# Two more block-product pairs in an FFN's last projection, with their weight sums made earlier

## The chip, the cores and the metric

The kernel runs on one core of a Trainium2 chip. A core has five engines that work at the same time: TensorE (PE in the profile) multiplies matrices, VectorE (DVE) and ScalarE (ACT) do elementwise work, GpSimd (POOL) does elementwise work and can issue transfers, and SyncE (SP) issues most transfers. Each engine takes its instructions strictly in order; where one waits, all behind it on that engine wait too. The metric is the device time of one execution in microseconds (us), a median over runs.

## The reference

One layer of a streaming encoder on x of 512 tokens by 1024 features: a combined projection, an attention branch and a recurrent branch, a gated merge, and then the FFN, all in float32.

```python
hn = rmsnorm(h, norm_ffn_g[l])
gu = hn @ w_ffn_in[l]                      # 1024 -> 2 x 2816
g, up = jnp.split(gu, 2, axis=-1)
h = h + (jax.nn.silu(g) * up) @ w_ffn_out[l]   # 2816 -> 1024
return rmsnorm(h, final_norm_g)
```

The change concerns the last product, (silu(g) * up) @ w_ffn_out: 2816 = 22 tiles of 128 rows of w_ffn_out, taken as 11 pairs of two tiles.

## The kernel before

Float32 products are made from two reduced-precision parts. Every operand is split into a high part (ScalarE, L82: a copy that rounds) and a low part (VectorE, L83: the value less its high part), and a product takes three matmuls (L76 to L78, `mm3`): high by high, high by low, low by high. So each weight tile that arrives in a `raw` tile costs one ScalarE and one VectorE instruction before TensorE can read it as `whl`.

Some products are taken as block products, in the manner of Winograd's form of Strassen's scheme: the tokens, the inner dimension and the columns are halved, and seven products of half blocks, of sums of blocks, take the place of eight. In the FFN's last projection a pair of tiles holds the two inner halves. A plain pair takes 2 tiles x 4 token tiles x 2 column halves x 3 = 48 matmuls of 512 columns, a block-product pair 7 x 2 x 3 = 42. Before, pairs 0 to 4 are plain and 5 to 10 are block products (`N_PLAIN`). The block products need sums of weight blocks, t1 = b12 - b11, t2 = b22 - t1, t3b = b22 - b12 and t4 = b21 - t2 (`out_sums`, L223, L225, L231, L237: VectorE, 128 partitions x 512 each), and sums of activation blocks (`a_sums`, L1442 to L1445). Before, all of them are made in the last stage, between the matmuls that use them.

The stages that the change touches, in order of time:

- The loop over the recurrent branch (66 to 130 us): projections `xr`, `gr`, `ga`, `gb`, the causal convolution `xc` (VectorE, three taps, L725), the recurrence gates `rg` on TensorE (L759), which read `xch`, a low part that GpSimd makes of `xc` (L730). The tiles b0 to b3 of the pool `obp` hold blocks of another weight, w_o, whose sums are made there and kept in DRAM.
- The FFN units fg0, fu0, fg1, fu1, fg2, fu2 (to about 727 us): each is a block product over seven weight kinds in the order w11, t1, t2, w22, t3, w21, t4, with the sums t1, t2, t3, t4 made by VectorE (L352, L367, L373). The results of a unit `fu` multiply those of `fg` (`sg`), partly on GpSimd, and are transposed for the last projection.
- The last projection (728 us to the end): first column half (`po_out0`, `p_out`), then the second, then the final norm.

The order of TensorE is written out by hand in the FFN and in the last projection, that of VectorE in the loop and in the last projection; elsewhere a scheduler merges the engines' instructions. The order of the DMA queues follows the order of issue. The pool `tg` has two tiles; it holds only short-lived scratch.

Of the kernel before, what the change touches and what calls it, by code (L numbers as in the profile page):

```python
# [14 lines left out]
P = 128  # L15
# [18 lines left out]
N_PLAIN = 5  # L34
PAIR_TILES = 2 * (11 - N_PLAIN)


@with_exitstack
def block_kernel(ctx: ExitStack, tc: tile.TileContext, x, norm_mix_g, w_in, b_merge, rel_table,
# [103 lines left out]
    for i in plain[:-3]:  # L143
        plan_out(1, i)
    for i in paired:
        plan_block("t12", i)
    plan_out(1, plain[-3])
# [11 lines left out]
    def load(name, k):  # L159
# [4 lines left out]
        raw = wp.tile([P, n, wide], F32, tag="raw", bufs=3, name=f"raw_{name}_{k}")  # L164
# [12 lines left out]
    t2_of, t2_room = {}, []  # L177
# [17 lines left out]

    def out_sums(name, rows):

        kind, i = name.split("_")
        if kind == "t4":
# [5 lines left out]
        def half_row(col):  # L205
            o = out_room[0].tile([P, S], F32, tag="half", bufs=3, name=f"half_{name}")
            sp.dma_start(out=o[:], in_=w_ffn_out[rows + P:rows + 2 * P, col:col + S])
            return o[:]

        if kind == "t12":  # L210
            raw = wp.tile([P, 2, S], F32, tag="raw", bufs=3, name=f"raw_{name}")
            sp.dma_start(out=raw[:], in_=w_ffn_out[rows:rows + P, :].rearrange("p (c n) -> p c n", c=2))
            b22 = half_row(S)

            if len(t2_of) < 2:
                if not t2_of:
                    t2_room.append(spare[0].tile([P, 2, S], F32, tag="act", bufs=13, name="t2_room"))
                t2 = t2_room[0][:, len(t2_of)]
            else:
                t2 = out_room[0].tile([P, S], F32, name=f"t2_{i}")[:]  # L220
            t2_of[i] = t2
            t1 = raw[:, 1]
            dve.tensor_sub(t1, raw[:, 1], raw[:, 0])  # L223
            low_parts()
            dve.tensor_sub(t2, b22, t1)  # L225
            high_first(hl[:, 0, 1], hl[:, 1, 1], t1)
            high_first(hl[:, 0, 0], hl[:, 1, 0], t2)
        elif kind == "t3b":
            raw = wp.tile([P, 2, S], F32, tag="raw", bufs=3, name=f"raw_{name}")
            sp.dma_start(out=raw[:], in_=w_ffn_out[rows:rows + 2 * P, S:].rearrange("(k p) n -> p k n", p=P))  # L230
            dve.tensor_sub(raw[:, 0], raw[:, 1], raw[:, 0])  # L231
            low_parts()
# [626 lines left out]
    for j in range(0, KT, 2):  # L859
# [7 lines left out]
        if j:  # L867
            gates_of(j)
# [771 lines left out]
```

## Time and profile before

| what | value |
|---|---|
| time, median of 3 runs | 849.77 us (849.75 to 851.16) |
| the profiled execution | 849.69 us, span 847.9 us |
| TensorE busy | 839.1 us, 99% of the span, clock 0.999 |
| VectorE busy | 663.2 us, 78% |
| ScalarE busy | 522.5 us, 62% |
| GpSimd busy | 140.6 us, 17% |
| DMA | 137.17 MB, mean 162 GB/s |

The span is what the profiler recorded from the first to the last instruction; 849.69 - 847.9 = 1.8 us lie outside it. In rows of single instructions the columns are start (us), duration (us), engine, line, operation, the tile written and the tiles read, the shapes, and in brackets the idle time of the engine before the instruction with what ended it. A TensorE row lasts longer than the step to the next row, since matmuls overlap; the step between starts is what a matmul costs.

### The profile page before, as it was taken

Reading aid. Unit: us, or ns where it says so; the run is one execution under the profiler, and the core shown is the slowest. Engines: PE = TensorE matmul, PEld = TensorE weight load, DVE = VectorE, ACT = ScalarE, POOL = GpSimd, SP = SyncE. Lnnn points to the kernel's source line nnn. Section 1 sums busy time; section 2 is a strip of 40 time slices with the busy share of each in tenths; the row PEclk is TensorE's granted clock in tenths of the full one; section 3 lists DMA queues with packets and bytes.
Section 4 is the critical chain, followed back from the end, with each engine's and each line's share of the span. In section 5 each row is a group of like instructions: output and inputs, shape, how many; then the busy total and the mean of one; then the engine's idle time right before and its main releaser. Section 6 shows DMA issues by size and latency. Waiting matters only on the chain.

```text
span 847.9 us, 11598 instructions
## 1 busy us (share of the span) xinstructions
PE 839.1 (99%) x4114; PEld 710.8 (84%) x4114; DVE 663.2 (78%) x972; ACT 522.5 (62%) x864; POOL 140.6 (17%) x179
## 2 busy tenths in 40 slices
PE   9999999999999999999999999999999999999996
PEld 6988888888888888888888888888888999888885
DVE  6667769886999788787568777888778878798995
ACT  7595848774466688787534568654664576645434
POOL 2412030221050133333000000003002213200000
PEclk9999999999999999999999999999999999999999
DMA  8433386777545433222233974555544445526642
GB/s 284 167 104 118 128 298 234 221 266 247 186 137 150 112 100 101 87 75 75 64 110 125 342 295 132 187 163 159 161 152 148 132 138 178 162 75 210 211 137 99
DMA packets 95385, 137.17 MB, mean 162 GB/s; under 512 B 7288, under 2 KB 62160, under 8 KB 94816
## 3 DMA queue, kind: packets, MB, share of 16 engines
q1 hardware_dynamic: 93696, 132.93, 48.9%
q10 hardware_dynamic: 1232, 2.95, 0.9%
q8 instruction: 32, 0.52, 0.3%
q0 software_dynamic: 400, 0.57, 0.3%
q14 instruction: 25, 0.20, 0.1%
HBM read 122.75 MB, written 13.67 MB: 161 GB/s over the span
## 4 chain that ended last, share of the span: by engine, by line
PE 82%; DVE 8%; ACT 4%; DMA 3%; issue 2%; ACTq 0%; DVEq 0%
PE fu_x L78 2%; PE fu_x L76 2%; PE fu_x L77 2%; PE po_out L76 2%; PE po_out L77 2%; PE po_out L78 2%; PE o L1088 2%; PE fg_x L78 2%; PE fg_x L76 2%; PE fg_x L77 2%; PE pT L1068 2%; PE po_ga L78 2%; PE po_ya L78 2%; PE po_ya L77 2%; PE po_ya L76 2%
## 5 line engine op out<-in xcount | busy, mean ns | idle before, releaser
L1288 POOL TENSOR_TENSOR sg<-sg,keep_fu_x 128x512 f32<-128x512 f32 (+1 forms) x10 | 17.8, 1782 | 238.8 <-DVE keep_fu_x L1287 238.8
L1057 POOL TENSOR_SCALAR p<-p,rl 128x128 f32<-128x128 f32 (+3 forms) x61 | 44.0, 739 | 14.9 <-DVE rl L1053 14.0
L1051 DVE CUSTOM_DVE_ANT_0 p<-s,bias 128x128 f32<-128x128 f32 (+1 forms) x64 | 28.6, 485 | 11.6 <-PE s L1043 10.2
L1052 ACT ACTIVATE p<-p,m 128x128 f32<-128x128 f32 (+1 forms) x64 | 35.5, 556 | 2.4 <-DVE m L1051 2.0
L76 PE MATMUL po_out<-whl_fo,act_hi 128*128 128x512 f32 (+1 forms) x80 | 30.9, 386 | 0.0
L78 PE MATMUL po_out<-whl_fo,act_lo 128*128 128x512 f32 (+1 forms) x80 | 30.7, 384 | 0.0
L77 PE MATMUL po_out<-whl_fo,act_hi 128*128 128x512 f32 (+1 forms) x80 | 30.7, 384 | 0.0
L83 DVE TENSOR_TENSOR whl_fu_w<-raw_fu_w,whl_fu_w 128x1024 fp32r<-128x1024 f32 (+1 forms) x18 | 22.1, 1227 | 8.5 <-ACT whl_fu_w L82 8.5
L83 DVE TENSOR_TENSOR pp<-pT,pp 128x384 fp32r<-128x384 f32 (+1 forms) x48 | 26.9, 596 | 2.0 <-ACT pp L82 1.8
L77 PE MATMUL po_xr<-xnT,whl_xr 128*128 128x512 f32 (+1 forms) x80 | 27.7, 353 | 0.0
L83 DVE TENSOR_TENSOR whl_fu_t<-t_fu,whl_fu_t 128x1024 fp32r<-128x1024 f32 (+1 forms) x18 | 23.8, 1324 | 4.8 <-ACT whl_fu_t L82 4.6
L77 PE MATMUL po_gr<-xnT,whl_gr 128*128 128x512 f32 (+1 forms) x80 | 27.5, 347 | 0.0
L78 PE MATMUL po_gr<-xnT,whl_gr 128*128 128x512 f32 (+1 forms) x80 | 27.3, 347 | 0.0
L78 PE MATMUL po_xr<-xnT,whl_xr 128*128 128x512 f32 (+1 forms) x80 | 27.2, 346 | 0.0
L76 PE MATMUL po_gr<-xnT,whl_gr 128*128 128x512 f32 (+1 forms) x80 | 27.1, 347 | 0.0
L76 PE MATMUL po_xr<-xnT,whl_xr 128*128 128x512 f32 (+1 forms) x80 | 26.3, 351 | 0.4 <-ACT xnT L615 0.4
L83 DVE TENSOR_TENSOR whl_fo<-raw_fo,whl_fo 128x1024 fp32r<-128x1024 f32 x16 | 20.7, 1304 | 7.7 <-ACT whl_fo L82 7.7
L82 ACT ACTIVATE whl_fu_w<-raw_fu_w 128x1024 fp32r<-128x1024 f32 (+1 forms) x18 | 17.8, 989 | 13.0 <-issue 7.1
L76 PE MATMUL po_k<-xnT,whl_qk 128*128 128x512 f32 x64 | 25.5, 398 | 0.0
L76 PE MATMUL po_q<-xnT,whl_qk 128*128 128x512 f32 x64 | 25.5, 398 | 0.0
L76 PE MATMUL po_ga<-xnT,whl_ga 128*128 128x512 f32 x64 | 25.4, 397 | 0.0
L82 ACT ACTIVATE whl_fu_t<-t_fu 128x1024 fp32r<-128x1024 f32 (+1 forms) x18 | 17.7, 988 | 12.6 <-PE fu_x L78 9.0
(614 smaller groups left out, 2994.9 us busy)
## 6 DMA issues: line engine op xcount, KB each, us to landing
raw_qk<-in_w_in_dram SPq DMA_DIRECT2D x32, 256.0 KB, 3.2
raw_fu_w<-in_w_ffn_in_dram SPq DMA_DIRECT2D x16, 512.0 KB, 4.4
raw_fo<-in_w_ffn_out_dram SPq DMA_DIRECT2D x16, 512.0 KB, 4.1
raw_xr<-in_w_in_dram SPq DMA_DIRECT2D x8, 512.0 KB, 5.7
raw_gr<-in_w_in_dram SPq DMA_DIRECT2D x8, 512.0 KB, 4.4
raw_ga<-in_w_in_dram SPq DMA_DIRECT2D x8, 512.0 KB, 3.8
raw_gb<-in_w_in_dram SPq DMA_DIRECT2D x8, 512.0 KB, 3.6
o_b<-in_w_o_dram SPq DMA_DIRECT2D x8, 512.0 KB, 6.9
```

Source lines behind the costliest of these rows:

```text
L76: pe.matmul(o, sh, mh, start=start, stop=False, skip_group_check=parts)
L77: pe.matmul(o, sh, ml, start=False, stop=False, skip_group_check=parts)
L78: pe.matmul(o, sl, mh, start=False, stop=stop, skip_group_check=parts)
L82: act.activation(hi, src, AF.Copy)
L83: dve.tensor_sub(lo, src, f(hi))
L1051: dve.tensor_tensor_reduce(prob[qb][:], scs[qb][:, 0:w], bias[:, S - w:S], -1.0, 3e38, ALU.add, ALU.min, nmax[:, qb:qb + 1])
L1052: act.activation(prob[qb][:], prob[qb][:], AF.Exp, bias=nmax[:, qb:qb + 1], scale=-1.0, accum_out=lsum[:, qb:qb + 1])
L1057: eng.tensor_scalar(prob[qb][:], prob[qb][:], rl[:, qb:qb + 1], 1.0, ALU.mult, ALU.mult)
L1068: pe.transpose(pt[:, at * P:(at + 1) * P], prob[qb][:, kb * P:(kb + 1) * P], ident[:])
L1088: pe.matmul(po[:, S - n:S], st, pp[i][:, part, lo:lo + n], start=kb == 0 and part == 0, stop=kb == NT - 1 and part == 1)
L1288: (pool if keep and (unit != f_units[-1] or side) else dve).tensor_mul(o, o, keep[a] if keep else banks[a])
```

## The change

Pairs 3 and 4 become block products too, so that eight of eleven pairs are. The weight sums of all eight pairs are no longer made in the last projection but earlier, and kept in DRAM (`out_t3` to `out_t10`, two 128 x 1024 tiles each, holding t4, t2 and t3b, t1):

- for pairs 3 to 6 in the recurrent loop, two pairs at j = 0 and two at j = 2, in the tiles b0 to b3, with 512 KB loads and stores on SP's queue (`out_pairs_kept`): 16 VectorE instructions of 128x512;
- for pairs 7 to 10 in the units fu0, fg1, fu1 and fg2, half a pair at a time, in the two `tg` tiles, with 256 KB loads and stores on GpSimd's queue (`out_half`, called after the product kinds that `spare_at` lists): 32 VectorE instructions of 128x256 and 32 transfers. Each call makes and stores the sums of the half before and then issues the loads of the next into the same two tiles.

The last projection then loads the sums instead of making them. The order of the pairs' products changes with it (`two_sided` puts off the second products of the last three pairs), the third sum's products go in groups of two and six, splits of activations are spread differently, ScalarE's order is written by hand there too, and two of the tiles for split activations come from the pool `sums_room`.

```diff
-N_PLAIN = 5
-PAIR_TILES = 2 * (11 - N_PLAIN)
+N_PLAIN = 3
+PAIR_TILES = 2 * (11 - N_PLAIN) - (4 - (N_PLAIN - 1))
...
+    out_kept = {i: dr.tile([2, P, D], F32, name=f"out_t{i}") for i in paired}
+    out_raw, t4_raw = [], {}
+    to_keep = list(paired)
+
+    def out_blocks(tiles, i, at=every, queue=sp):
+
+        for n, raw in enumerate(tiles):
+            rows = (2 * i + n) * P
+            queue.dma_start(out=raw, in_=w_ffn_out[rows:rows + P, :].rearrange("p (c n) -> p c n", c=2)[:, :, at])
+        out_raw.append((tiles, i, at))
+
+    def out_sums_kept(queue=sp):
+
+        (one, two), i, at = out_raw.pop(0)
+        tc.keep_in_program_order(dve.tensor_sub(one[:, 1], one[:, 1], one[:, 0]))
+        dve.tensor_sub(two[:, 1], two[:, 1], one[:, 1])
+        dve.tensor_sub(one[:, 0], two[:, 1], one[:, 0])
+        dve.tensor_sub(two[:, 0], two[:, 0], two[:, 1])
+        for n, raw in enumerate((one, two)):
+            queue.dma_start(out=out_kept[i][n].rearrange("p (c n) -> p c n", c=2)[:, :, at], in_=raw)
...
+    def out_half():
+
+        if out_raw:
+            out_sums_kept(pool)
+        if halves_left or to_keep:
...
+            tiles = [tg_.tile([P, 2, CW], F32, tag="tg", name=f"half_out{i}_{at.start}_{n}")[:] for n in range(2)]
+            out_blocks(tiles, i, at, pool)
...
         if kind == "t12":
...
-            dve.tensor_sub(t1, raw[:, 1], raw[:, 0])
             low_parts()
-            dve.tensor_sub(t2, b22, t1)
...
+            sp.dma_start(out=raw[:], in_=out_kept[i][:, :, S:].rearrange("c p n -> p c n"))
+        elif kind == "t3b":
+            sp.dma_start(out=raw[:, 0], in_=out_kept[i][0, :, 0:S])
+            sp.dma_start(out=raw[:, 1], in_=w_ffn_out[rows + P:rows + 2 * P, S:])
...
+    def out_pairs_kept():
+        for tags in (("b0", "b1"), ("b2", "b3")):
+            out_blocks([f(obp.tile([P, 2, S], F32R, tag=tag, name=f"{tag}_out{to_keep[0]}")[:]) for tag in tags], to_keep.pop(0))
+        for _ in range(2):
+            out_sums_kept()
...
+        if j == 2:
+            out_pairs_kept()
...
             if j == w == 0:
                 gates_of(j)
+                out_pairs_kept()
...
+    spare_at = {"fu0": ("w11", "t1", "t4"), "fg1": ("t1", "t4"), "fu1": ("t1", "t4"), "fg2": ("t1", "t4")}
...
         f_product(fz, unit, "t1", True)
         kept(z1, fz)
+        spare_work("t1")
```

VectorE in the loop at j = 2, just ahead of the convolution `xc2` (`whl_ga2` is a split weight, `u0` the recurrence of the step before). Before:

```order
L792 SCALAR_TENSOR_TENSOR u0_690<-u0_690,g1_598 128x512
L725 SCALAR_TENSOR_TENSOR xc2_830<-po_xr2_0_805,vc_164,xc2_830 128x511
L725 SCALAR_TENSOR_TENSOR xc2_830<-po_xr2_0_805,vc_164,xc2_830 128x510
L725 SCALAR_TENSOR_TENSOR xc2_830<-po_xr2_0_805,vc_164,xc2_830 128x509
L83 TENSOR_TENSOR whl_ga2_0_795<-raw_ga2_0_796,whl_ga2_0_795 128x1024
L83 TENSOR_TENSOR whl_ga2_4_800<-raw_ga2_4_801,whl_ga2_4_800 128x1024
L725 SCALAR_TENSOR_TENSOR xc3_863<-po_xr2_1_838,vc_164,xc3_863 128x511
L725 SCALAR_TENSOR_TENSOR xc3_863<-po_xr2_1_838,vc_164,xc3_863 128x510
L725 SCALAR_TENSOR_TENSOR xc3_863<-po_xr2_1_838,vc_164,xc3_863 128x509
```

And now:

```order
L817 SCALAR_TENSOR_TENSOR u0_698<-u0_698,g1_606 128x512
L215 TENSOR_TENSOR b0_out3_731<-b0_out3_731 128x512
L216 TENSOR_TENSOR b1_out3_732<-b1_out3_732,b0_out3_731 128x512
L217 TENSOR_TENSOR b0_out3_731<-b1_out3_732,b0_out3_731 128x512
L218 TENSOR_TENSOR b1_out3_732<-b1_out3_732 128x512
L215 TENSOR_TENSOR b2_out4_735<-b2_out4_735 128x512
L750 SCALAR_TENSOR_TENSOR xc2_858<-po_xr2_0_833,vc_172,xc2_858 128x511
L216 TENSOR_TENSOR b3_out4_736<-b3_out4_736,b2_out4_735 128x512
L750 SCALAR_TENSOR_TENSOR xc2_858<-po_xr2_0_833,vc_172,xc2_858 128x510
L83 TENSOR_TENSOR whl_ga2_0_823<-raw_ga2_0_824,whl_ga2_0_823 128x1024
L217 TENSOR_TENSOR b2_out4_735<-b3_out4_736,b2_out4_735 128x512
L218 TENSOR_TENSOR b3_out4_736<-b3_out4_736 128x512
```

Eight subtractions (L215 to L218, on the b tiles of pairs 3 and 4) stand ahead of and between the taps of `xc2`.

VectorE in the unit fg1, from the sum t2 to the split of w22. Before:

```order
L352 TENSOR_TENSOR t2_fg1_0_5580<-raw_fg1_t2_110_5578,t1_fg1_0_5478 128x1024
L352 TENSOR_TENSOR t2_fg1_1_5584<-raw_fg1_t2_111_5582,t1_fg1_1_5486 128x1024
L83 TENSOR_TENSOR whl_fg1_t2_0_5576<-t2_fg1_0_5580,whl_fg1_t2_0_5576 128x1024
L83 TENSOR_TENSOR whl_fg1_t2_1_5577<-t2_fg1_1_5584,whl_fg1_t2_1_5577 128x1024
L83 TENSOR_TENSOR whl_fg1_w22_0_5629<-raw_fg1_w22_110_5631,whl_fg1_w22_0_5629 128x1024
L83 TENSOR_TENSOR whl_fg1_w22_1_5630<-raw_fg1_w22_111_5633,whl_fg1_w22_1_5630 128x1024
L367 TENSOR_TENSOR raw_fg1_t3_000_5680<-t2_fg1_0_5580,raw_fg1_t3_000_5680 128x1024
L367 TENSOR_TENSOR raw_fg1_t3_001_5683<-t2_fg1_1_5584,raw_fg1_t3_001_5683 128x1024
```

And now (`half_out7_256` is the second half of pair 7, `half_out8_0` the first half of pair 8):

```order
L377 TENSOR_TENSOR t2_fg1_1_5656<-raw_fg1_t2_111_5654,t1_fg1_1_5548 128x1024
L217 TENSOR_TENSOR half_out7_256_0_5378<-half_out7_256_1_5379,half_out7_256_0_5378 128x256
L218 TENSOR_TENSOR half_out7_256_1_5379<-half_out7_256_1_5379 128x256
L83 TENSOR_TENSOR whl_fg1_t2_0_5648<-t2_fg1_0_5652,whl_fg1_t2_0_5648 128x1024
L83 TENSOR_TENSOR whl_fg1_t2_1_5649<-t2_fg1_1_5656,whl_fg1_t2_1_5649 128x1024
L83 TENSOR_TENSOR whl_fg1_w22_0_5711<-raw_fg1_w22_110_5713,whl_fg1_w22_0_5711 128x1024
L215 TENSOR_TENSOR half_out8_0_0_5584<-half_out8_0_0_5584 128x256
L83 TENSOR_TENSOR whl_fg1_w22_1_5712<-raw_fg1_w22_111_5715,whl_fg1_w22_1_5712 128x1024
L392 TENSOR_TENSOR raw_fg1_t3_000_5762<-t2_fg1_0_5652,raw_fg1_t3_000_5762 128x1024
L392 TENSOR_TENSOR raw_fg1_t3_001_5765<-t2_fg1_1_5656,raw_fg1_t3_001_5765 128x1024
L216 TENSOR_TENSOR half_out8_0_1_5585<-half_out8_0_1_5585,half_out8_0_0_5584 128x256
L398 TENSOR_TENSOR t2_fg1_0_5652<-raw_fg1_w21_100_5815,t2_fg1_0_5652 128x1024
```

The last sums of one half stand ahead of the split of t2, and the first subtraction of the next half stands between the two splits of w22, four VectorE rows later.

GpSimd at the same place. Before:

```order
L1288 TENSOR_TENSOR sg0_2_4889<-sg0_2_4889,keep_fu0_z1_5247 128x512
L1288 TENSOR_TENSOR sg0_3_4890<-sg0_3_4890,keep_fu0_z1_5247 128x512
L1288 TENSOR_TENSOR sg0_0_4887<-sg0_0_4887,keep_fu0_x1_5245 128x512
L1288 TENSOR_TENSOR sg0_1_4888<-sg0_1_4888,keep_fu0_x1_5245 128x512
L1288 TENSOR_TENSOR sg1_01_5517<-sg1_01_5517,keep_fu1_x2_5856 128x512
```

And now:

```order
L1321 TENSOR_TENSOR sg0_0_4935<-sg0_0_4935,keep_fu0_x1_5293 128x512
L1321 TENSOR_TENSOR sg0_1_4936<-sg0_1_4936,keep_fu0_x1_5293 128x512
L220 DMA out_t7_96<-half_out7_256_0_5378 256x1x256
L220 DMA out_t7_96<-half_out7_256_1_5379 256x1x256
L209 DMA half_out8_0_0_5584<-in_w_ffn_out_dram 128x2x256
L209 DMA half_out8_0_1_5585<-in_w_ffn_out_dram 128x2x256
L220 DMA out_t8_97<-half_out8_0_0_5584 256x1x256
L220 DMA out_t8_97<-half_out8_0_1_5585 256x1x256
```

Between the products of fu0 and those of fu1, where it had nothing to do, it now issues the stores of one half, then the loads of the next into the same tiles, then its stores; each load waits for the store of the same tile to be complete.

VectorE in the last projection, where the weights t1 and t2 of the second column half (`whl_t12`) are prepared. Before:

```order
L223 TENSOR_TENSOR raw_t12_7_7208<-raw_t12_7_7208 128x512
L189 TENSOR_TENSOR whl_t12_6_7122<-raw_t12_6_7123,whl_t12_6_7122 128x512
L189 TENSOR_TENSOR whl_t12_6_7122<-t2_room_7105,whl_t12_6_7122 128x512
L225 TENSOR_TENSOR t2_7_7212<-half_t12_7_7210,raw_t12_7_7208 128x512
L223 TENSOR_TENSOR raw_t12_8_7220<-raw_t12_8_7220 128x512
L189 TENSOR_TENSOR whl_t12_7_7207<-raw_t12_7_7208,whl_t12_7_7207 128x512
L189 TENSOR_TENSOR whl_t12_7_7207<-t2_7_7212,whl_t12_7_7207 128x512
L225 TENSOR_TENSOR t2_8_7224<-half_t12_8_7222,raw_t12_8_7220 128x512
L223 TENSOR_TENSOR raw_t12_9_7232<-raw_t12_9_7232 128x512
```

And now:

```order
L1491 TENSOR_TENSOR s_8_7261<-act8_6593 128x256
L1492 TENSOR_TENSOR s_8_7261<-s_8_7261,act8_6593 128x256
L1493 TENSOR_TENSOR act8_6593<-act8_6593 128x256
L1494 TENSOR_TENSOR act8_6593<-act8_6593,s_8_7261 128x256
L83 TENSOR_TENSOR right8_7260<-s_8_7261,right8_7260 128x2x256
L194 TENSOR_TENSOR whl_t12_4_7229<-raw_t12_4_7230,whl_t12_4_7229 128x1024
L194 TENSOR_TENSOR whl_t12_5_7268<-raw_t12_5_7269,whl_t12_5_7268 128x1024
L194 TENSOR_TENSOR whl_t12_6_7273<-raw_t12_6_7274,whl_t12_6_7273 128x1024
L1491 TENSOR_TENSOR s_9_7296<-act9_6594 128x256
L1492 TENSOR_TENSOR s_9_7296<-s_9_7296,act9_6594 128x256
```

The sums L223 and L225 are gone there; a split is one 128x1024 instruction, and the activation sums of the later pairs stand among them.

More of the change, by code (lines that the diff above doesn't have):

```diff
@@ L142, in block_kernel @@
         plan_out(0, i)
-    for i in plain[:-3]:
+    for i in plain[:-2]:
         plan_out(1, i)
@@ L203, in out_sums @@
             hl = out_home(name)
[L205 to L208, printed above, removed]
-        if kind == "t12":
[L211 to L223, printed above, removed]
-            low_parts()
-            dve.tensor_sub(t2, b22, t1)
[L226 to L232, printed above, removed]
-            high_first(hl[:, 0], hl[:, 1], raw[:])
-        else:
-            b21 = half_row(0)
-            t2 = t2_of[i]
-            dve.tensor_sub(t2, b21, t2)
-            low_parts()
-            high_first(hl[:, 0], hl[:, 1], t2)
@@ L1407, in block_kernel @@
         gated(unit, 0, 1, fz, x2)
+        spare_work("w22")
         turn()
```

136 lines of the change are left out of this document (102 added, 34 removed).

## The prediction

> **What bounds the kernel now.** The page first: busy shares and the chain of work that ended last.
>
> ```profile
> span 847.9 us, 11598 instructions
> PE 839.1 (99%) x4114; PEld 710.8 (84%) x4114; DVE 663.2 (78%) x972; ACT 522.5 (62%) x864; POOL 140.6 (17%) x179
> ...
> PE 82%; DVE 8%; ACT 4%; DMA 3%; issue 2%; ACTq 0%; DVEq 0%
> ```
>
> TensorE is busy for 99% and carries the chain. So a removed matmul is worth its step, as long as no operand becomes late, and VectorE's work costs only where it makes an operand late. The step is read from the timeline of TensorE in the last projection: a plain pair, then a block-product pair.
>
> ```profile
> 745.86 0.39 PE L76 MATMUL po_out<-whl_fo,act_hi 128*128 128x512 f32 x1
> ...
> 748.58 0.39 PE L76 MATMUL po_out<-whl_fo,act_hi 128*128 128x512 f32 x1
> ...
> 756.74 0.39 PE L76 MATMUL p_out<-whl_fo,left 128*128 128x512 f32 x1
> ...
> 759.46 0.39 PE L76 MATMUL p_out<-whl_fo,left 128*128 128x512 f32 x1
> ```
>
> From 745.86 to 748.58 lie 12 steps, from 756.74 to 759.46 another 12: both 2.72 us, 0.227 us each. A block-product matmul costs what a plain one does.
>
> **The change part by part.**
>
> *Matmuls.* Two pairs go from 48 to 42 matmuls: 12 fewer, 12 x 0.227 = **-2.72 us**. TensorE's order is the same up to the last projection, so all else can only add to that, by waits.
>
> *The last projection: sums away, splits earlier.* In VectorE's groups from 728 to 840 us, by form:
>
> ```profile
> L223 DVE TENSOR_TENSOR raw_t<-raw_t 128x512 f32<-128x512 f32 x6 | 4.1, 688 | 1.4 <-DMA raw_t<-in_w_ffn_out_dram 1.3
> L231 DVE TENSOR_TENSOR raw_t3b<-raw_t3b 128x512 f32<-128x512 f32 x6 | 4.1, 683 | 0.0
> ```
>
> With L225 and L237, which have the same shape, 24 sums of 0.69 us go: 16.5 us of VectorE. But the block products begin earlier: in the first column half a plain pair takes 24 steps (5.44 us), a block-product pair 12. They start after three plain pairs, at 745.9 in place of 756.7, and the `left` of the last of eight pairs is read 72 steps later, at 762.2. Is VectorE ready?
>
> ```profile
> 736.87 1.23 DVE L83 TENSOR_TENSOR whl_fo<-raw_fo,whl_fo 128x1024 fp32r<-128x1024 f32 x1 [4.56 <-ACT whl_fo L82]
> 738.01 1.22 DVE L1377 TENSOR_TENSOR act_lo<-act,act_hi 128x1024 fp32r<-128x1024 f32 x1
> 739.14 0.68 DVE L83 TENSOR_TENSOR left<-act,left 128x512 fp32r<-128x512 f32 x1
> 739.75 0.42 DVE L1442 TENSOR_TENSOR s<-act 128x256 f32<-128x256 f32 x1
> ...
> 741.94 0.69 DVE L83 TENSOR_TENSOR left<-act,left 128x512 fp32r<-128x512 f32 x1
> ```
>
> The steps are 1.14 for a weight split, 0.61 for a `left`, 2.19 for a set of activation sums with its `right`. ScalarE's transposed activations still end there, which lets VectorE begin at 736.9. Up to the last `left` it then has 8 weight splits (9.1), 8 `left` (4.9), 3 sets (6.6) and 2 additions to h (1.2): 21.8 us, done at 758.7, against 762.2. The second half loses the 24 sums, so I give this stage **0**; if a load is late there, VectorE's margin of 3.5 us is what is eaten first.
>
> *The loop.* Sixteen subtractions of 128x512 are added, at 0.61 us a step (a two-input form of that shape, as `left`): 4.9 us in each of two places. VectorE, then GpSimd and TensorE behind it:
>
> ```profile
> 67.32 0.69 DVE L792 SCALAR_TENSOR_TENSOR u<-u,g 128x512 f32<-128x512 f32 x1
> 69.37 2.32 DVE L725 SCALAR_TENSOR_TENSOR xc<-po_xr,vc,xc 128x511 f32<-128x511 f32 x3 [1.37 <-ACT xc L718]
> ...
> 73.40 1.66 DVE L83 TENSOR_TENSOR whl_ga<-raw_ga,whl_ga 128x1024 fp32r<-128x1024 f32 x1 [0.58 <-ACT whl_ga L82]
> 74.98 2.31 DVE L725 SCALAR_TENSOR_TENSOR xc<-po_xr,vc,xc 128x511 f32<-128x511 f32 x3
> 78.53 0.69 DVE L742 SCALAR_TENSOR_TENSOR g<-g,po_gr 128x512 f32<-128x512 f32 x1 [1.24 <-ACT g L741]
> ...
> 86.83 0.69 DVE L747 SCALAR_TENSOR_TENSOR g<-g,po_gr 128x512 f32<-128x512 f32 x1
> 89.52 0.69 DVE L786 SCALAR_TENSOR_TENSOR gt<-gt,xc 128x512 f32<-128x512 f32 x1 [2.00 <-ACT gt L771]
> ```
>
> ```profile
> 78.15 1.29 POOL L730 TENSOR_TENSOR xch<-xc,xch 128x512 fp32r<-128x512 f32 x1 [4.17 <-issue]
> ```
>
> ```profile
> 82.14 1.32 PE L759 MATMUL rg<-xch,wrg 64*128 64x512 f32 x10
> ```
>
> The first eight find 1.4 us of idle time before 69.37, 0.6 before 73.40, and about 0.6 where steps between dependent rows and the slowed row at 73.40 shrink, so the second `xc` ends 2.3 us later, at 79.6, GpSimd's `xch` ends at 81.8 in place of 79.4, and `rg` starts at 82.14: still 0.4 to 1.3 us in time, as the first of the ten or the later ones need it. The idle 1.24 before 78.53 and those behind it take up the rest; the second eight find 2.00 before 89.52. I take **0**; the cost without this cover is at most some 2 us.
>
> *The FFN units.* Per half, four subtractions of 128x256 (0.42 us by the row at 739.75, less the overlap of rows that don't depend on one another), some 1.5 us of VectorE in idle time. What costs is order: the first subtraction of a half stands between the two splits of w22, and waits for a load that waits for the last half's store. In fg1:
>
> ```profile
> 592.39 1.23 DVE L83 TENSOR_TENSOR whl_fg_t<-t_fg,whl_fg_t 128x1024 fp32r<-128x1024 f32 x1
> ...
> 597.06 1.23 DVE L83 TENSOR_TENSOR whl_fg_w<-raw_fg_w,whl_fg_w 128x1024 fp32r<-128x1024 f32 x1 [1.52 <-ACT whl_fg_w L82]
> 598.86 1.22 DVE L83 TENSOR_TENSOR whl_fg_w<-raw_fg_w,whl_fg_w 128x1024 fp32r<-128x1024 f32 x1 [0.57 <-ACT whl_fg_w L82]
> ...
> 604.56 1.23 DVE L373 TENSOR_TENSOR t_fg<-raw_fg_w,t_fg 128x1024 f32<-128x1024 f32 x1 [1.08 <-DMA raw_fg_w<-in_w_ffn_in_dram]
> ...
> 625.51 1.22 DVE L83 TENSOR_TENSOR whl_fu_w<-raw_fu_w,whl_fu_w 128x1024 fp32r<-128x1024 f32 x1
> ```
>
> ```profile
> 628.54 0.39 PE L77 MATMUL fu_x<-whl_fu_w,hn 128*128 128x512 f32 x1
> ```
>
> The third subtraction ends about 593.5 (where the row at 592.39 starts, plus 1.1 us of added ones), and its store may go. The next half is wanted at 598.3. Round trips (store issued to load landed) up to 4.8 us cost nothing. Beyond, the split at 598.86 is late, with it the load into the raw tile that this split frees, the sum at 604.56, and a chain nearly without gaps through VectorE and ScalarE to the split at 625.51, done 1.8 us before TensorE reads it at 628.54. With the few small gaps on the way I count 2.9 us, less 0.7 for two added subtractions: 2.2 us. So the wait reaches TensorE in fg1 from a round trip of 4.8 + 2.2, about 7.1 us with signals. In fu1:
>
> ```profile
> 632.51 1.23 DVE L352 TENSOR_TENSOR t_fu<-raw_fu_t,t_fu 128x1024 f32<-128x1024 f32 x1 [0.35 <-DMA raw_fu_t<-in_w_ffn_in_dram]
> ...
> 639.62 1.23 DVE L83 TENSOR_TENSOR whl_fu_w<-raw_fu_w,whl_fu_w 128x1024 fp32r<-128x1024 f32 x1 [0.57 <-ACT whl_fu_w L82]
> ...
> 644.01 1.23 DVE L373 TENSOR_TENSOR t_fu<-raw_fu_w,t_fu 128x1024 f32<-128x1024 f32 x1 [0.90 <-DMA raw_fu_w<-in_w_ffn_in_dram]
> ...
> 647.43 1.22 DVE L83 TENSOR_TENSOR whl_fu_t<-raw_fu_t,whl_fu_t 128x1024 fp32r<-128x1024 f32 x1
> ```
>
> ```profile
> 650.30 0.39 PE L77 MATMUL fu_x<-whl_fu_t,bts 128*128 128x512 f32 x1
> ```
>
> The slack is 650.30 - 648.65 and the gap of 0.90, 2.5 us, less three added subtractions: 1.5. The third subtraction ends at 632.5, the next half is wanted at 639.0: a threshold of 8.0 us. In fg2:
>
> ```profile
> 670.16 2.07 DVE L83 TENSOR_TENSOR whl_fg_t<-t_fg,whl_fg_t 128x768 fp32r<-128x768 f32 x2
> ...
> 680.52 0.96 DVE L373 TENSOR_TENSOR t_fg<-raw_fg_w,t_fg 128x768 f32<-128x768 f32 x1 [1.02 <-DMA raw_fg_w<-in_w_ffn_in_dram]
> ```
>
> There the first subtraction stands two rows later, at about 678.4; the third one before ends near 671.9. With the gap of 1.02 and an estimated 1.5 us further on the threshold is about 9.
>
> What does a round trip take? No row is a 256 KB transfer on GpSimd's queue. The nearest:
>
> ```profile
> raw_fo<-in_w_ffn_out_dram SPq DMA_DIRECT2D x16, 512.0 KB, 4.1
> ...
> raw_v_t<-in_w_in_dram SPq DMA_DIRECT2D x16, 256.0 KB, 3.2
> ...
> out_dram<-hg SPq DMA_DIRECT2D x4, 320.0 KB, 2.2
> ...
> g_fin<-in_final_norm_g_dram POOLq DMA_DIRECT2D x1, 512.0 KB, 5.3
> ```
>
> From below, by SP's rows: 2.2 + 3.2 = 5.4, no wait. From above, twice GpSimd's own row: 10.6. Between: SP's 256 KB load and a store of about 2.5, each with up to 5.3 - 4.1 = 1.2 for the queue, 5.7 to 8.1. I take 7.6, as the queue is the new thing: a wait of 7.6 - 7.1 = **+0.5** in fg1, none in fu1 and fg2.
>
> The Trainium skill ("DMA: Bandwidth & Descriptors", Anatomy of one DMA) has a fit for this very queue, about 2.0 us plus bytes over 436 GB/s: 2.6 us for 256 KB, by which the estimate is 5.2 for the round trip, no wait and 847.0. This trace's one such row is 5.3 us at 512 KB where the fit gives 3.2, so I don't go by it. The same page (SWDGE vs HWDGE vs iDMA) sends plain transfers to SP or ScalarE, since descriptors made in software start later; that speaks against this change, and g_fin's row agrees in sign.
>
> **Sum.** 849.69 - 2.72 + 0.5 = 847.47. The profiled execution lies 0.08 below the median. **Forecast 847.5 us**.
>
> **Rivals.**
>
> *Half the gain is lost to the round trips.* At 8.1 to 9.3 us, fg1 waits 1.0 to 2.2 and fu1 0.1 to 1.3, fg2 up to 0.3: 848.1 to 850.8, 849.4 in the middle. For it: g_fin. Against: g_fin moves twice the bytes. Chance 0.22.
>
> *Slower: the queue is as slow as its own row.* At 10.6, fg1 waits 3.5, fu1 2.6, fg2 1.6, together 7.7: **854.7 us**. It decides from a round trip of 9.5, where the waits are 2.4 + 1.5 + 0.5 = 4.4 and eat the gain and the 0.2% below. Against it: SP's 256 KB rows, and that GpSimd, busy for 17% of the span, is mostly free. Chance 0.18.
>
> *The loop is late.* If the b tiles' loads land late, among 512 KB stores that stand ahead of weight loads on SP's queue, VectorE waits in order at `xc`; 2 us more than its margin give 848.5 to 849.5. For it: 8 MB of added transfers near 100 us. Against: weight loads there go out long before use, and TensorE has no gap now. Chance 0.08.
>
> *All of it is had*, 847.0, with a round trip under 7.1: this is the forecast's own lower edge.
>
> **How the numbers follow.** The forecast, 846.9 to 848.1, has 0.52. A measurement of this kernel can tell about 0.2%, 1.7 us, from no change: below 848.07 is faster. That is the forecast, 0.51 of it, and little of the loop case: 0.52. Slower, above 851.5: the slow queue, 0.18. Between: 0.30. The range 846.8 to 852.5 leaves out the slow queue's upper part and little below.
>
> **What would show it.** Right: 12 TensorE instructions fewer; block products from about 746 us; no idle time of TensorE near 82, 610 and 640; GpSimd's 256 KB issues landing after 3.5 to 4 us; VectorE's wait for `half_out` in fg1 of some 2 to 3 us, nearly all of it taken up before TensorE. Wrong: a landing of over 4.7 us a transfer and TensorE gaps in fg1, fu1 and fg2, each later by the same; gaps at `rg` in the loop; or a gap in the last projection at `left` or `whl_t12`, which would fell the 0 that I gave it.

## The result, and the profile after the change

The changed kernel took **855.88 us** (median; 853.37 to 859.47), the kernel before, beside it on the same chip, 849.91. The ratio is 1.0067, with a 95% interval of 1.0047 to 1.0088: slower by 5.7 us by the ratio, where 847.5 had been forecast, and outside the predicted range. In what follows a difference of 0.001 in such a ratio is 0.85 us.

The first lines of the page after the change:

```profile
span 854.0 us, 11741 instructions
...
PE 839.8 (98%) x4102; PEld 708.2 (83%) x4102; DVE 680.2 (80%) x1008; ACT 522.1 (61%) x868; POOL 165.4 (19%) x211
```

TensorE has its 12 instructions fewer, but it is no longer busy without a break: the span grew by 6.1 us. To see where, the matmuls of the two traces were put side by side in order (they are the same up to the last projection), and for each the start before was subtracted from the start after. By the clock of the trace before, this lateness is 0.1 us from 8 us on, 0.7 at 83, 1.5 at 163, 2.9 at 231, 3.8 at 249, 4.4 at 480, 4.8 at 587, 6.5 at 611, 7.5 at 650 and 8.6 at 707. It stays there through the last projection until the 12 missing matmuls take 2.7 off. So about half of it is there when the FFN begins, most of that before the attention's heads, the rest arises in the FFN units, and the last projection adds none.

**The loop, first eight subtractions.** VectorE's timeline after the change (start, duration, engine, line, operation, output<-inputs):

```profile
67.91 0.69 DVE L215 TENSOR_TENSOR b_out<-b_out 128x512 f32<-128x512 f32 x1
68.63 1.68 DVE L216 TENSOR_TENSOR b_out<-b_out,b_out 128x512 f32<-128x512 f32 x1
70.34 1.67 DVE L217 TENSOR_TENSOR b_out<-b_out,b_out 128x512 f32<-128x512 f32 x1
71.94 0.68 DVE L218 TENSOR_TENSOR b_out<-b_out 128x512 f32<-128x512 f32 x1
...
79.19 2.31 DVE L750 SCALAR_TENSOR_TENSOR xc<-po_xr,vc,xc 128x511 f32<-128x511 f32 x3
```

GpSimd's in the same stretch:

```profile
67.07 4.39 POOL L822 TENSOR_TENSOR rnn<-u,rnn 128x512 fp32r<-128x512 f32 x2 [7.21 <-ACT rnn L821]
...
82.35 1.29 POOL L755 TENSOR_TENSOR xch<-xc,xch 128x512 fp32r<-128x512 f32 x1 [1.93 <-issue]
```

The first of these rows before the change:

```profile
67.08 3.33 POOL L797 TENSOR_TENSOR rnn<-u,rnn 128x512 fp32r<-128x512 f32 x2 [7.21 <-ACT rnn L796]
```

And TensorE's after it:

```profile
82.19 1.09 PE L784 MATMUL rg<-xch,wrg 64*128 64x512 f32 x8
83.70 0.50 PE L784 MATMUL rg<-xch,wrg 64*128 64x512 f32 x2 [0.42 <-POOL xch L755]
```

Two of the four subtractions take 1.67 us in place of 0.69: they run beside GpSimd's two `rnn` operations, and those take 4.39 us together, where the same row before the change (L797) had 3.33. The same two lines take 0.68 us at 73.80 and 76.19, where GpSimd is idle. The Trainium skill ("SBUF — State Buffer", SBUF: two separate sides) says that a VectorE operation with two inputs in SBUF and a GpSimd operation that reads SBUF take a shared pair of ports under an exclusive lock, so that the second waits for the first. Two of these rows agree in kind; the first subtraction, at 67.91, was not slowed although GpSimd's row had begun, and no run here shows the lock itself. The second `xc` then ends at 81.5, `xch` at 83.6, and the last two of TensorE's ten `rg` wait for it.

**The loop, second eight.** They are late for another reason:

```profile
103.00 1.23 DVE L318 TENSOR_TENSOR o_b<-o_b,o_b 128x1024 f32<-128x1024 f32 x1 [1.15 <-DMA o_b<-in_w_o_dram]
...
119.15 2.31 DVE L750 SCALAR_TENSOR_TENSOR xc<-po_xr,vc,xc 128x511 f32<-128x511 f32 x3
```

The same `xc` before:

```profile
111.79 2.32 DVE L725 SCALAR_TENSOR_TENSOR xc<-po_xr,vc,xc 128x511 f32<-128x511 f32 x3 [0.43 <-ACT xc L718]
```

The blocks of w_o go into the tiles from which the second pairs' sums are stored, so their loads wait for those stores, and VectorE waits in order for the load, 1.15 us here. It reaches the `xc` of that place 7.4 us later than before (119.15 against 111.79); experiments 11 and 12 take that apart. At 230.7, where the attention's first scores need VectorE, its rows are still 3.9 us later than before, and TensorE's lateness grows from 1.5 to 2.9 and soon to 3.8. Not all of that growth is the loop's: in the trace of experiment 1, which makes no early sums at all, the same VectorE row is 1.6 us later than before, and TensorE's lateness is 0.6 us there and 1.4 at 249.

**The FFN.** VectorE's list of waits from 540 to 735 us (us in total, times, longest), after the change, begins with a line that was not there before:

```profile
DVE half_out L215 <- DMA half_out<-in_w_ffn_out_dram: 8.4, 2, 5.7
```

In fg1, on VectorE and then on GpSimd, whose queue carries the halves:

```profile
598.25 0.41 DVE L218 TENSOR_TENSOR half_out<-half_out 128x256 f32<-128x256 f32 x1
...
601.98 1.23 DVE L83 TENSOR_TENSOR whl_fg_w<-raw_fg_w,whl_fg_w 128x1024 fp32r<-128x1024 f32 x1 [0.62 <-ACT whl_fg_w L82]
608.91 0.43 DVE L215 TENSOR_TENSOR half_out<-half_out 128x256 f32<-128x256 f32 x1 [5.71 <-DMA half_out<-in_w_ffn_out_dram]
609.25 1.22 DVE L83 TENSOR_TENSOR whl_fg_w<-raw_fg_w,whl_fg_w 128x1024 fp32r<-128x1024 f32 x1
```

```profile
598.73 1.44 POOL L220 DMA_DIRECT2D out_t<-half_out  x2 [8.23 <-DVE half_out L218]
604.54 0.72 POOL L209 DMA_DIRECT2D half_out<-in_w_ffn_out_dram  x1 [4.38 <-DMA out_t<-half_out]
```

Read the two together: the stores are issued at 598.73, the next load goes when the first has landed (604.54, 5.8 us later), and the subtraction that needs that load begins at 608.91 (4.4 us). A round trip of 10.2 us, and all of it after the first split of w22 is VectorE's wait: 5.71 us, with the second split of w22 queued behind it. In fu1 the same rows give 8.7 us (store issued 639.62, subtraction at 648.34) and a wait of 2.69. In fg2 a round trip is 6.5 us. The list has no wait for it, because it puts the two waits there, 1.00 and 1.76 us, down to other causes; but by the trace the loads of the two tiles landed at 686.95 and 690.00, just ahead of these rows:

```profile
687.03 0.43 DVE L215 TENSOR_TENSOR half_out<-half_out 128x256 f32<-128x256 f32 x1 [1.00 <-DVE raw_fg_t L392]
...
690.09 0.42 DVE L216 TENSOR_TENSOR half_out<-half_out,half_out 128x256 f32<-128x256 f32 x1 [1.76 <-issue]
```

TensorE pays with a wait in fg1:

```profile
617.33 0.50 PE L77 MATMUL fg_x<-whl_fg_t,bts 128*128 128x512 f32 x1 [1.20 <-DVE whl_fg_t L83]
```

In fu1 it waits at 657.8, at the end of a run of VectorE rows without a gap that begins with the wait of 2.69, and is 1.0 us later behind it. In fu2, at 715.8, it loses another 1.1 us, but there no subtraction waits. TensorE waits for a split that VectorE reached late and that took 3.23 us beside a GpSimd operation, where the same split, also beside one, took 2.22 before:

```profile
712.50 3.23 DVE L83 TENSOR_TENSOR whl_fu_t<-t_fu,whl_fu_t 128x768 fp32r<-128x768 f32 x1 [0.65 <-ACT whl_fu_t L82]
```

```profile
712.30 2.62 POOL L1410 TENSOR_TENSOR act_lo<-act,act_hi 128x1024 fp32r<-128x1024 f32 x1
```

How much of this 1.1 us comes from the waits in fg2 and how much from the slower split is not shown.

### The profile page after: what moved, and what is told of

Its sections match the earlier page's. It is cut to its first block, busy times and chain, and to the rows that moved or that the text cites. A ratio compares the mean times of both kernels' runs of the same rounds, so it can differ in the third digit from the quotient of the medians.

```text
span 854.0 us, 11741 instructions
## 1 busy us (share of the span) xinstructions
PE 839.8 (98%) x4102; PEld 708.2 (83%) x4102; DVE 680.2 (80%) x1008; ACT 522.1 (61%) x868; POOL 165.4 (19%) x211
## 4 chain that ended last, share of the span: by engine, by line
PE 67%; DVE 11%; DMA 9%; issue 7%; ACT 5%; POOL 1%; ACTq 0%; DVEq 0%; POOLq 0%
PE o L1121 2%; PE pT L1101 2%; DMA half_out<-in_w_ffn_out_dram 2%; PE po_ya L76 2%; PE po_q L76 2%; PE po_k L76 2%; PE po_q L77 2%; PE po_ya L77 2%; PE po_q L78 2%; PE p_out L77 2%; PE p_out L76 2%; PE po_k L77 2%; PE po_k L78 2%; PE po_ya L78 2%; PE p_out L78 2%
## 5 line engine op out<-in xcount | busy, mean ns | idle before, releaser
L220 POOL DMA_DIRECT2D out_t<-half_out x16 | 11.3, 736 | 123.9 <-DVE half_out L218 123.8
L209 POOL DMA_DIRECT2D half_out<-in_w_ffn_out_dram x16 | 11.8, 736 | 116.6 <-ACT hj L1235 96.8
L729 POOL MEMSET bias<- 64x64 f32 x16 | 2.4, 148 | 125.7 <-DMA bias<-ext_d 125.7
L76 PE MATMUL po_ga<-xnT,whl_ga 128*128 128x512 f32 x64 | 25.4, 397 | 0.0
L76 PE MATMUL po_gb<-xnT,whl_gb 128*128 128x512 f32 x64 | 25.2, 394 | 0.0
L78 PE MATMUL po_ga<-xnT,whl_ga 128*128 128x512 f32 x64 | 25.0, 391 | 0.1
L77 PE MATMUL po_ga<-xnT,whl_ga 128*128 128x512 f32 x64 | 25.0, 390 | 0.0
```

What stands on the lines that cost most here:

```text
L76: pe.matmul(o, sh, mh, start=start, stop=False, skip_group_check=parts)
L77: pe.matmul(o, sh, ml, start=False, stop=False, skip_group_check=parts)
L78: pe.matmul(o, sl, mh, start=False, stop=stop, skip_group_check=parts)
L209: queue.dma_start(out=raw, in_=w_ffn_out[rows:rows + P, :].rearrange("p (c n) -> p c n", c=2)[:, :, at])
L220: queue.dma_start(out=out_kept[i][n].rearrange("p (c n) -> p c n", c=2)[:, :, at], in_=raw)
```

## The experiments

The theory was that the loss has two places, the loop and the halves, and that the matmul gain itself is had. Each ratio is to the kernel before, run beside it. Where sums are left out, the block products are fed with the plain blocks of the weights.

**1 to 3: none of the early sums, the halves alone, the loop's sums alone.** The edits, in this order:

```diff
 def out_half():          # 1 and 3
+    return
 def out_pairs_kept():    # 1 and 2
+    to_keep.pop(0), to_keep.pop(0)
+    return
```

> Leaves out all the early weight sums: nothing is made in the loop or in the FFN units, and the last projection loads plain weight blocks of the same shapes where the kept sums would be, so its result is not the reference's; matmuls, splits and loads of the last projection are as in the changed kernel. Theory: the last projection has the full gain and no new wait, and all the loss lies ahead of it: before less 12 matmuls, 849.8 - 2.7 = about 847.1. Rival: the earlier start of the block products costs something there too: 848.5 or more, with TensorE gaps after 735 us.

> Leaves out the sums of pairs 3 to 6 in the loop with their 512 KB transfers (the last projection loads plain blocks in their place; wrong result); the halves of pairs 7 to 10 in the FFN units stay. Theory: the loop's 16 subtractions make VectorE late for good, and TensorE's lag of 4.4 us at 480 us in the changed kernel's trace is theirs: about 855.9 - 4.4 = 851.5, with no lag at 480 us. Rival: the lag would be taken up later anyway, or comes from DMA traffic of the whole: 853.5 or more.

> Leaves out the sums of pairs 7 to 10 in the FFN units with their 256 KB transfers on GpSimd's queue (plain blocks in their place; wrong result); the loop's sums stay. Theory: the FFN's share of the lag, 8.6 - 4.4 = 4.2 us, goes: about 851.7, with the lag of 4.4 us at 480 us unchanged. Rival: part of the FFN's lag is the loop's lateness handed on: 853 or more.

Measured: 0.997 (0.9953 to 0.9986) with neither, 1.0025 (1.0011 to 1.004) with the halves, 1.0014 (1.0004 to 1.0025) with the loop's sums. So the 12 matmuls are worth 0.0030 (2.5 us, against 2.72 worked out), the halves cost 0.0055 (4.7 us) and the loop's sums 0.0044 (3.7 us). The three add up to +0.0069, and the whole change measured +0.0067: two losses and one gain that add, as far as intervals of 0.001 to 0.002 on each ratio can tell. In the trace of the third, TensorE's lateness is 4.0 us at 249 us, 4.4 at 480, and does not grow through the FFN. The second came out between its theory and its rival (median 852.97), and its lag did not go: its trace, that of the slowest of its ten executions, is 2.0 us late at 249. With the 1.4 of the first this says that single traces differ by 1 to 2 us at the start of the attention even without sums in the loop, so the costs above are taken from the ratios.

**4: the halves at other places.** The first subtraction of a half moved from the calls after t1 to those after t3; the t4 sums of the FFN were pinned in VectorE's order, so that the calls had a place of their own.

```diff
-    spare_at = {"fu0": ("w11", "t1", "t4"), "fg1": ("t1", "t4"), "fu1": ("t1", "t4"), "fg2": ("t1", "t4")}
+    spare_at = {"fu0": ("w11", "t1", "t3", "t4"), "fg1": ("t3", "t4"), "fu1": ("t3", "t4"), "fg2": ("t3",)}
```

> The changed kernel with its halves spread over the FFN units (after w11, t1, t3, t4 in fu0, after t3 and t4 in fg1 and fu1, after t3 in fg2), so that between the last subtraction of one half and the first of the next lie 12 us or more, and none is left for fu2; same sums, same transfers, same queue. Theory (VectorE waits in order for a round trip of 9 to 10.5 us through GpSimd's queue): the waits of 5.7 and 2.7 us and the 1.1 us of fu2 go, and with them most of 4.2 us: about 852.3. Rival (the added VectorE work or the traffic itself, wherever it stands, makes the FFN late): 855 or more.

Measured: 1.0141 (1.0119 to 1.0162); the expectation of 852.3 fell. The waits for `half_out` are gone from the head of VectorE's list, and the time is worse. Busy time by stretch of that kernel (length, then busy us and number of instructions of TensorE, its weight loads, VectorE, ScalarE and GpSimd, the granted clock, the DMA share and GB/s):

```profile
571.00:603.00 32.00, 29.18 (x126) 23.72 (x125) 29.83 (x32) 10.59 (x13) 14.39 (x13) 0.95 0.62 201
```

VectorE is busy for 29.83 of 32 us (27.01 before the change): the subtractions now fall where the next unit's w11 is due, and TensorE has a gap of 2.83 us at 595.6. It is confounded by the pinned t4 sums, so it says no more than that these places were worse.

**5 and 6: the halves' stores left out; the halves on SP's queue.**

```diff
         for n, raw in enumerate((one, two)):       # 5; pairs 7 to 10 then read plain blocks
+            if queue is pool:
+                continue
-            out_sums_kept(pool)                    # 6
+            out_sums_kept()
-            out_blocks(tiles, i, at, pool)
+            out_blocks(tiles, i, at)
```

> Leaves out the stores of the halves of pairs 7 to 10 (the last projection loads plain blocks in their place; wrong result); their loads, their subtractions and the loop stay. The load of a half then waits for VectorE alone, and the round trip shrinks from 8.7 to 10.5 us to one load, about 4.8 us. Theory (the waits of VectorE for the round trip are what costs in fg1 and fu1): TensorE's lag grows by about 1.5 us in the FFN in place of 4.2, with 1.1 of it in fu2: 853.2. Rival (the 32 subtractions cost it by their own time): the growth stays 3.5 us or more, 855 or above.

> The changed kernel with the halves' loads and stores on SP's queue in place of GpSimd's; nothing is left out. Theory: the round trip is set by the completion of a store to DRAM and a load, of which the queue is a part of some 1 us each; at 7 to 8 us it falls under most of the slack, and the FFN's 4.2 us shrink to about 2: 853.7. Rival: SP waits in order for each store, so the weight loads queued behind it come late, and the time is 856 or more.

Measured: 1.0065 (1.004 to 1.009) without the stores, 1.0054 (1.0035 to 1.0073) on SP's queue; neither can be told from the change itself, and both theories (853.2 and 853.7) fell. For the first, VectorE in fg1 shows why (the trace is of one of its slower executions, 858.8 against a median of 855.5):

```profile
603.77 0.43 DVE L215 TENSOR_TENSOR half_out<-half_out 128x256 f32<-128x256 f32 x1 [3.13 <-DMA half_out<-in_w_ffn_out_dram]
...
605.37 2.35 DVE L83 TENSOR_TENSOR whl_fg_w<-raw_fg_w,whl_fg_w 128x1024 fp32r<-128x1024 f32 x2
...
612.97 1.22 DVE L405 TENSOR_TENSOR t_fg<-raw_fg_w,t_fg 128x1024 f32<-128x1024 f32 x1 [2.97 <-DMA raw_fg_w<-in_w_ffn_in_dram]
```

Without the stores the load goes at 598.0 and lands at 603.3, but the scheduler, which only the first subtraction's place binds, now puts all four ahead of both splits of w22. The wait is shorter (3.13), holds up both splits, and so the raw tile that they free and the load into it: 2.97 us more at 612.97. The wait changed its form and stayed.

For the second, the medians from issue to landing, in SP's queue and then, in the change itself, in GpSimd's:

```profile
half_out<-in_w_ffn_out_dram SPq DMA_DIRECT2D x16, 256.0 KB, 3.6
out_t<-half_out SPq DMA_DIRECT2D x16, 256.0 KB, 2.7
```

```profile
half_out<-in_w_ffn_out_dram POOLq DMA_DIRECT2D x16, 256.0 KB, 4.1
out_t<-half_out POOLq DMA_DIRECT2D x16, 256.0 KB, 3.7
```

A store and a load together are 6.3 us in the one and 7.8 in the other. The queue is faster by 1.5 us, and no difference in the time can be told. The profiled execution on SP's queue (852.58) lies 3 us below the median of its runs; in it VectorE's wait in fg1 is 4.10 us in place of 5.71, and TensorE's lateness grows by only 1.0 us in the FFN. So a gain in some executions is not ruled out.

**7 and 8: the sums in the attention.** Eight halves of pairs 3 to 6, or all sixteen halves, go into tiles of their own beside every second head, or beside every head, in place of the loop's sums, or of all; SP's queue carries them.

```diff
+    eo_stack, eo = opened("eo", 2)
+            if h in range(1, 16, 2):      # 8: range(16), and spare_at = {}
+                half_in()
+            if h in range(1, 16, 2):
+                out_sums_kept()
```

> The sums of pairs 3 to 6 move from the recurrent loop to the attention stage, half a pair in every second head, in two tiles of their own, with loads and stores on SP's queue; pairs 7 to 10 stay in the FFN units as in the changed kernel. Theory (VectorE has idle time in every head there, and rows wait 3 us or more before TensorE needs them): the loop's 3.6 us go and nothing comes in their place: 852.3. Rival (any added VectorE work between GpSimd's instructions is slowed, and attention waits for it): 854.5 or more.

> All eight pairs' sums in the attention stage, half a pair in each of the 16 heads, on SP's queue; nothing in the loop or in the FFN units; the result is the reference's. Theory: 1.5 us of VectorE in each head of 13.5 us fit its idle time of 2 us or more, and the gain of the block products is kept: 847.2 to 848.2, below the kernel before. Rival: the idle time is needed to take up GpSimd's slowing of VectorE, and heads run late by 0.5 us or more each: 852 or more.

Measured: 1.0068 (1.0042 to 1.0093) and 1.0121 (1.0106 to 1.0137). Both theories (852.3, and 847.2 to 848.2) fell. With eight, the lateness at 249 us is 1.4 in place of 3.8, the same as without any early sums, so the loop's loss is gone, but 1.7 us come up at the heads until 381 us; what the loop got back was paid in the attention. With sixteen, the busy time by stretch, before the change and with the sums there:

```profile
360.00:380.00 20.00, 20.00 (x112) 17.58 (x112) 15.99 (x39) 16.07 (x39) 6.67 (x12) 1.00 0.28 80
```

```profile
360.00:380.00 20.00, 18.28 (x99) 15.53 (x98) 18.12 (x44) 14.02 (x34) 5.26 (x10) 1.00 0.62 184
```

VectorE rises from 80% to 91% and TensorE loses 1.7 of 20 us. TensorE's waits from 300 to 420 us are for VectorE's and GpSimd's softmax work:

```profile
PE po_q L76 <- DVE m L1095: 2.8, 2, 1.5
PE pT L1112 <- POOL p L1101: 2.8, 6, 1.3
```

VectorE's own list of that stretch has waits of the FFN's kind again:

```profile
DVE half_out L215 <- DMA half_out<-in_w_ffn_out_dram: 5.3, 4, 1.6
DVE half_out L216 <- DMA half_out<-in_w_ffn_out_dram: 2.4, 3, 1.0
```

So the sums do not fit into the attention as they were placed there, though VectorE's share of busy time over the whole span is only 78%. Whether their own time or their waits for loads cost more is not shown: no run here makes them there without transfers.

**9 and 10: is it the halves' transfers, their subtractions, or the wait?** Both have no sums in the loop. The first makes all the halves' transfers and no subtraction; a mark that VectorE sets where the first subtraction stood lets GpSimd store them. The second makes all 32 subtractions on one pair of tiles that is loaded once.

```diff
 def out_sums_kept(queue=sp):                       # 9
-    ... the four subtractions
+    tc.keep_in_program_order(dve.memset(fill_[:, n:n + 1], 0.0))
+    for t in (one, two):
+        pool.tensor_copy(t[:, 0, 0:1], fill_[:, n:n + 1])
 def out_sums_kept(queue=sp):                       # 10, behind the four subtractions
+    out_raw.append(((one, two), i, at))
+    return
```

> The FFN's halves without their 32 subtractions: they are loaded and stored as they were, the store let go by a mark of one element per partition that VectorE sets where the first subtraction stood (it waits for nothing) and that GpSimd copies into both tiles; no sums in the loop (pairs 3 to 6 are loaded plain). Measured against the version with the halves whole and no loop sums (1.0025) and the one without any early sums (0.997). Theory, VectorE waits in order for a round trip: nothing waits on VectorE now, so all is had, 0.997 (0.996 to 0.998). Rival, the 8 MB of transfers delay the weight loads of the FFN: most of the loss stays, 1.001 to 1.0025, with raw_fg and raw_fu landing later. Rival, VectorE's time: 0.997 too, told apart by the next run.

> The other half of the same question: one pair of tiles is loaded once in the first FFN unit and the 32 subtractions are made on it over and over, at the same calls; no further loads and no stores, no loop sums. The block products load plain weights. VectorE has its added 13 us but nothing to wait for. Theory, the wait for the round trip is the cost: 0.997 to 0.9985, of which 0.001 is what the subtractions themselves cost where VectorE has no gap. Rival, VectorE's added time is the cost, wait or none: 1.0015 to 1.0025. If both this and the run before lie near 0.997, the two are only a loss together, which is the wait.

Measured: 0.9972 (0.9961 to 0.9982) and 0.9959 (0.9945 to 0.9973), against 0.997 without early sums and 1.0025 with whole halves. Each alone costs nothing that can be told; together 0.0055. (In the second the scheduler puts all four subtractions of a half ahead of both splits of w22, as in 5, and still nothing is lost.) What only the two together have is a subtraction that waits for a transfer. In the trace of the first the halves' transfers are even slower than in the change:

```profile
half_out<-in_w_ffn_out_dram POOLq DMA_DIRECT2D x16, 256.0 KB, 4.2
out_t<-half_out POOLq DMA_DIRECT2D x16, 256.0 KB, 4.4
```

and TensorE is busy for all of the 195 us from 540 to 735. So neither the transfers nor VectorE's added work makes the halves' loss by itself; what is left is VectorE's wait in order, with what follows from it.

**11 and 12: the same question in the loop**, without halves. The subtractions cut to one column (and two of the four left out), all loads and stores kept; then all subtractions on tiles loaded once, no stores.

```diff
-        tc.keep_in_program_order(dve.tensor_sub(one[:, 1], one[:, 1], one[:, 0]))     # 11, and so on
+        tc.keep_in_program_order(dve.tensor_sub(one[:, 1, 0:1], one[:, 1, 0:1], one[:, 0, 0:1]))
 def out_pairs_kept():                                                                 # 12
-    for tags in (("b0", "b1"), ("b2", "b3")):
+    if not out_raw:
+        for tags in (("b0", "b1"), ("b2", "b3")):
```

> The loop's sums cut to one element per partition (two subtractions of 128x1 a pair in place of four of 128x512); all their loads and stores stay; no halves in the FFN. Against 1.0014 with whole sums and 0.997 with none. Theory, VectorE's time (4.9 us at each place, and more where GpSimd works beside it) makes xc late: 0.997 to 0.998. Rival, the 8 MB of transfers on SP's queue hold up the weight loads behind them: 1.000 to 1.0014, with VectorE waiting for raw weight tiles or o_b between 100 and 160 us.

> The loop's sixteen subtractions on tiles that are loaded once and never stored, at the same two places; no halves in the FFN; the block products load plain weights. Theory, VectorE's time: 1.000 to 1.0014. Rival, the transfers: 0.997 to 0.998. Between the two by equal parts: 0.999.

Measured: 0.9963 (0.9949 to 0.9977) with the transfers, 0.9987 (0.9977 to 0.9997) with the subtractions, against 0.997 with neither and 1.0014 with both. The transfers alone cost nothing. The subtractions alone cost 0.0017 (1.4 us); by the ratios this is not clear of the noise (the intervals of 0.9987 and of 0.997 overlap), but the trace has it at one place:

```profile
82.28 1.45 PE L792 MATMUL rg<-xch,wrg 64*128 64x512 f32 x8
84.42 0.50 PE L792 MATMUL rg<-xch,wrg 64*128 64x512 f32 x2 [0.68 <-POOL xch L763]
```

TensorE is 1.35 us late behind these rows, and no more than 2.3 us anywhere ahead of the missing matmuls. The rest, 0.0027 (2.3 us), needs both, and these intervals (1.0004 to 1.0025, 0.9977 to 0.9997) lie apart. The `xc` that stood at 111.79 before, with the transfers alone (11), the subtractions alone (12) and both (3):

```profile
112.35 2.32 DVE L754 SCALAR_TENSOR_TENSOR xc<-po_xr,vc,xc 128x511 f32<-128x511 f32 x3
```

```profile
114.91 2.30 DVE L758 SCALAR_TENSOR_TENSOR xc<-po_xr,vc,xc 128x511 f32<-128x511 f32 x3
```

```profile
120.56 2.31 DVE L756 SCALAR_TENSOR_TENSOR xc<-po_xr,vc,xc 128x511 f32<-128x511 f32 x3
```

It is late by 0.6, 3.1 and 8.8 us; only with both does a later `rg`, at 130.65 in experiment 3, wait 0.67 us for its `xch`. SP's queue in the kernel with the loop's sums whole (experiment 3), where each DMA issue has its start:

```profile
97.17 0.38 SPq L316 DMA_DIRECT2D o_b<-in_w_o_dram  x1
97.66 0.40 SPq L220 DMA_DIRECT2D out_t<-b_out  x1
98.60 0.38 SPq L316 DMA_DIRECT2D o_b<-in_w_o_dram  x1
...
105.90 0.37 SPq L316 DMA_DIRECT2D o_b<-in_w_o_dram  x1
```

and with the subtractions cut to a column (11):

```profile
91.34 4.55 SPq L314 DMA_DIRECT2D o_b<-in_w_o_dram  x4
```

Four loads of w_o go out at 91.3 to 95.9 where the sums are quick, and at 97.2 to 105.9 where whole sums make the stores late that must leave the tiles first. VectorE then waits 2.47 us at 104.8 for the first of them, in experiment 3, and 1.15 in the change. It is the FFN's mechanism again: sums, store, load into the same tile, and an engine in order behind it.

All runs but 4, 6, 7 and 8 leave sums or stores out, so their times are no offers. The four that compute the whole output are no faster than the change within their intervals, and none beats the kernel before.

## Why the prediction was wrong

- *Matmuls, -2.72 us*: **right**. 0.003 (2.5 us, give or take 1.4) without the early sums, and 2.7 us come off TensorE's lateness in the last projection.
- *The last projection, 0*: **right**. TensorE has no wait there after the change, though block products begin earlier, and its lateness does not grow there.
- *The loop, 0, "at most some 2 us" without cover*: **wrong**, 3.7 us. Two steps failed. The first took 0.61 us for each subtraction and let the second `xc` end at 79.6 and `xch` at 81.8; beside GpSimd's `rnn` two of them take 1.7 us, and the ends were 81.5 and 83.6. The ten `rg` were said to be "0.4 to 1.3 us in time"; that was less than this one error of 1.9 us. By the run with the subtractions alone it costs about 1.4 us. The second step looked for idle time (the 2.00 before 89.52) and not at the tiles: which load waits for the added stores was never asked for, though the prediction asked just that in the FFN. It is the remaining 2.3 us. The rival that the loop is late had its place among the stores on SP's queue, and a chance of 0.08; its price was 1 to 2 us, and its cause, loads landing late among stores, is not it: with all the transfers and no sums nothing is late. What was late was their issue, behind stores that wait for the sums.
- *The FFN, thresholds of 7.1, 8.0 and 9*: the mechanism, VectorE waiting in order at the subtraction ahead of the second split of w22, was **right**, and so was the distance: 10.2 - 4.8 = 5.4 us of wait in fg1, where the row says 5.71. The term that was mis-sized is the **round trip**, taken as 7.6: it was 10.2 in fg1, 8.7 in fu1 and 6.5 in fg2. The sum of medians (4.1 + 3.7 = 7.8) would have confirmed 7.6; it is the worst of them at the place with the least slack that counts. For 10.2, 8.7 and 6.5 the thresholds give 3.1, 0.7 and 0 us, 3.8 in all; TensorE's lateness grew by 1.5 in fg1, 1.0 in fu1, and 1.1 in fu2, which the prediction did not cost at all. So fg1 had more slack than was counted, and that the sums come out close is partly luck. In all the halves cost 4.7 us by the ratios, against +0.5.
- *The queue as the new thing*: **wrong in weight**. On SP's queue a store and a load are 1.5 us shorter by their medians, and over the runs the time is the same within the intervals. By the Trainium skill ("DMA: Bandwidth & Descriptors", Anatomy of one DMA), whose fit gave an estimate of 2.6 us for each of these transfers, no wait was expected; the rows have 4.1 and 3.7, and 2.7 to 3.6 on SP's queue. The measurement decides.
- *The chances*: the rival "the queue is as slow as its own row" (854.7, with waits in fg1, fu1 and fg2) and "the loop is late" were weighed as alternatives. Both happened at once, in part each, and no case had both. In the main they rest on the same thing, a tile that is stored before it is loaded again, so they should have been weighed together: +4.7 and +3.7 less 2.5 is 5.9, against 5.7 measured. That 854.7 lies near the measured 855.9 is luck in part: it left out the loop, and took 10.6 us in every unit.

## What to carry to other kernels

Work added to an engine that is free for a fifth of the span can cost little by its own time (13 us of VectorE in the FFN: nothing that could be measured; eight subtractions at a tight place in the loop: about 1.4 us), but an instruction that waits for a transfer, on an engine that works in order, stops all that is queued behind it. Count the distance from the store that frees a tile to the first use of its next content, at the place where it is shortest, and against the worst landing rather than the median; where the distance is short, neither a faster queue nor a dropped store changed the time here by anything that could be told. Ask of every tile that an added store reads which load comes into it next.

## What the runs showed of the hardware that was not expected

- VectorE's two-input subtraction of 128x512 took 0.68 us where GpSimd was idle, and 1.67 us in two rows beside a GpSimd operation on tensors of the same shape, two of which took 4.39 us in place of 3.33.
- 8 MB of added traffic in the FFN delayed no weight load so that TensorE noticed: from 540 to 735 us the DMA share is 0.51 before the change and 0.65 in the run with the transfers alone, where TensorE is busy for all of the 195 us.
- The same 256 KB store on GpSimd's queue took from issue to landing 3.7 us by the median, and 5.4 and 5.7 in fg1, the place where it mattered most.
